# Part 1, second half, of layer 2's output product: from direct matmuls to seven products of half size, mixed step by step with part 2's

## The chip, the cores and the metric

The kernel runs on one core of one Trainium2 chip. The metric is the device time of one execution in microseconds (us): the median of three runs is 2115.03 us (2114.95 to 2115.57). A profile was taken of one more execution, of 2114.73 us. Its traced span is 2113.0 us; 1.73 us lie outside the span.

## The reference, cut to what matters

Two decoder layers run over 512 tokens with 2048 features. Layer 1 mixes tokens by retention, layer 2 by latent attention. What the change touches is the last product of layer 2 and what follows it:

```python
y = (jax.nn.silu(g) * o) @ w_out        # layer 2: (512 x 2048) @ (2048 x 2048)
x = x + gate * y                        # residual, after the last layer
return rmsnorm(x, final_norm_g)
```

All of it is in float32.

## The kernel before

**Numbers.** TensorE is fed float32 values as two rounded parts, a high and a low one: ScalarE (ACT) casts the high part, VectorE (DVE) subtracts it from the value to get the low part. This pair of operations is `split`, L134 to L136. One product of a weight block with an activation block is three matmuls: high by high, high by low, low by high. In the ordinary form these three stand on L158, L159 and L160; in the form with seven products they stand on one line, L984.

**Tiling.** In `w_mla_out` the 2048 output columns are cut into four parts of T = 512; H = 256 is half of that and P = 128. The output is held transposed: a block of 128 output columns by 512 tokens fills one PSUM bank and has a number kt from 0 to 15; part r holds kt 4r to 4r+3. The inputs of the product are 16 k-tiles of 128 rows by 512 tokens, in eight units of two.

- Parts 0 and 1 (`for r in range(2)`, L2540) are computed directly. A unit u loads a weight block `o2_w{r}_{u}` of 2 k-tiles by 512 columns (512 KB) into one of three buffers with the tag "raw", splits it, and takes 2 k-tiles x 4 blocks x 3 = 24 matmuls of 512 columns of tokens.
- Part 2 (`o2_2`, made by `seven_rows_steps`, L966) uses the seven products of Strassen and Winograd in place of eight: the weights of a step are a 2 x 2 pattern (even and odd k-tiles, left and right 256 columns), the tokens are in two halves. Eight steps `00` to `03` and `10` to `13` follow one another. A step of the first four loads two tiles of 512 KB, `e` and `o`, forms differences on DVE (L1016, L1018, L1019), splits both tiles (L1017/L1020 and L1022/L1023) and takes four products of 12 matmuls of 256 columns (x, s, z, y). A step of the second four loads 768 KB, prepares them at L1028 to L1034, and takes three such products (x, y, s). Sums of the inputs, `o2_s` and `o2_t` of each of the eight input units, are formed earlier by `o2_sums` (L2408); four of the t sums are split later (`o2_late_sums`).
- Part 3 (`o2_3`, L2607) is direct again, with weight tiles `o2_w3_0` to `o2_w3_7`.

**Closing a block.** `o2_put` (L2471) adds the gated product to the residual on DVE (L2477), squares it and scales it on ACT, and adds the squares to a running sum `x2_ss` on DVE (L2489). The residual rows are loaded by `o2_residual` (L2431) into tiles `o2_xr{kt}`, five buffers with the tag "pp" for kt below 13. Finished blocks of part 1 stand in the list `waiting` and are put one by one (`put_one`).

**Order.** It is written by hand. Each engine has its queue of instructions and runs it in order. `chunk` and `run` issue load, preparation and matmuls of a unit; `o2_hooks(i)` adds other work at unit i, counted over parts 0 and 1 (16 units): sums of unit u at hook u+6, the loads of the first three steps of part 2 at hooks 13, 14 and 15. The loop at L2579 goes through the eight steps: the load of the step after the next two, some loads for part 3 (`loads3`) and one residual, all on SyncE's queue (SP), then the matmuls, then the preparation of the step after the next and the work in `work3`. Loads take their buffer by turns from the pool "bw" (two) and the pool "raw" (three), in `turns3`; a load into a buffer waits on SP until the last reader of the buffer has finished, and all that stands behind it on SP waits with it.

Of the kernel before, what the change touches and what calls it, by code (L numbers as in the profile page):

```python
# [49 lines left out]
def hybrid_trunk_kernel(  # L50
# [2402 lines left out]

# [332 lines left out]
```

## Time and profile before

| | |
|---|---|
| median of three runs | 2115.03 us (2114.95 to 2115.57) |
| profiled execution | 2114.73 us, span 2113.0 us |
| PE (matmuls) | 2098.4 us busy, 99% |
| PEld (weight loads) | 1814.2 us, 86% |
| DVE | 1680.8 us, 80% |
| ACT | 1054.1 us, 50% |
| POOL | 103.8 us, 5% |
| DMA | 465.08 MB, mean 220 GB/s |
| chain that ended last | PE 95%, DMA 3%, DVE 1% |
| part 1 direct (192 matmuls) | 1973.41 to 2016.93 |
| part 2, seven products (336 matmuls) | 2016.93 to 2055.32 |
| part 3 and the end | from 2055.32; span ends at 2113.0 |

Busy shares are means over the whole span. For one stage one reads the stretch of that stage: which engine has no gap in it, and what its rare gaps waited for. A matmul's row shows its own duration, but matmuls are pipelined, so a stream's pace is read from the distance of starts. DVE's rows overlap by some 0.08 us in the same way. SPq rows are issues of DMAs on SyncE's queue; the time from issue to landing stands in the DMA view.

### The profile page before, as it was taken

How to read it: one execution, taken by the hardware profiler on the slowest of the kernel's cores; microseconds unless marked ns; L12 is line 12 of the kernel's file. 1: busy time of each engine (PE TensorE's matmuls, PEld its weight loads, DVE VectorE, ACT ScalarE, POOL GpSimd, SP SyncE). 2: the span in 40 equal slices, each digit the busy share in tenths (PEclk: the TensorE clock that was granted, in tenths of full speed). 3: DMA queues.
4: the chain of work that ended last, by engine and by line, in shares of the span. 5: the costliest groups of instructions: out<-in, count | busy, mean ns of one | idle time of the engine just before them, and what ended most of it. 6: DMA issues, size and time to landing. Idle time of an engine off the chain costs nothing.

```text
span 2113.0 us, 30423 instructions
## 1 busy us (share of the span) xinstructions
PE 2098.4 (99%) x11268; PEld 1814.2 (86%) x11268; DVE 1680.8 (80%) x2562; ACT 1054.1 (50%) x1626; POOL 103.8 (5%) x177
## 2 busy tenths in 40 slices
PE   8999999999999999999999999999999999999998
PEld 6888898989889888888888888898889999888898
DVE  7999888888888789666777877767978788887675
ACT  6765444444444444434344445345446565665343
POOL 1001010000000000000000000010000000000000
PEclk9999999999999999999999999999999999999999
DMA  9975786868777778755656656753556655455453
GB/s 382 407 281 195 250 276 222 278 216 268 245 259 250 237 237 278 260 188 183 234 170 227 220 184 235 265 178 111 167 186 207 199 166 187 153 188 176 148 166 126
DMA packets 237303, 465.08 MB, mean 220 GB/s; under 512 B 21169, under 2 KB 91857, under 8 KB 233569
## 3 DMA queue, kind: packets, MB, share of 16 engines
q1 hardware_dynamic: 224512, 423.17, 60.5%
q0 software_dynamic: 11920, 38.91, 4.8%
q8 instruction: 88, 1.44, 0.3%
q10 hardware_dynamic: 722, 1.06, 0.2%
q14 instruction: 61, 0.50, 0.1%
HBM read 420.06 MB, written 43.00 MB: 219 GB/s over the span
## 4 chain that ended last, share of the span: by engine, by line
PE 95%; DMA 3%; DVE 1%; ACT 0%; SPq 0%; issue 0%; POOLq 0%; DVEq 0%
PE o L1486 16%; PE x L884 2%; PE x L883 2%; PE y L884 2%; PE y L883 2%; PE s L884 2%; PE s L883 2%; PE x L885 2%; PE s L885 2%; PE y L885 2%; PE o L2607 2%; PE qk L158 2%; PE s_qk L984 2%; PE x_qk L984 2%; PE qk L160 2%; PE qk L159 2%
## 5 line engine op out<-in xcount | busy, mean ns | idle before, releaser
L1486 PE MATMUL o<-o_h,o_p 128*128 128x512 f32 (+1 forms) x1088 | 322.9, 377 | 0.0
L1486 PEld LDWEIGHTS o<-o_h,o_p 128*128 128x128 f32 x1088 | 200.2, 188 | 37.1
L1486 PE MATMUL o<-o_l,o_p 128*128 128x512 f32 (+1 forms) x544 | 204.8, 377 | 0.0
L136 DVE TENSOR_TENSOR o_p<-o_r,o_p 128x1024 fp32r<-128x1024 f32 x64 | 78.1, 1221 | 52.5 <-ACT o_p L135 52.2
L1486 PEld LDWEIGHTS o<-o_l,o_p 128*128 128x128 f32 x544 | 102.3, 188 | 18.2
L1170 DVE SCALAR_TENSOR_TENSOR mod<-mod,c_odd 128x1024 f32<-128x1024 f32 x56 | 67.2, 1219 | 14.9 <-DMA mod<-in_ada_t_dram 14.9
L135 ACT CAST o_p<-o_r 128x1024 fp32r<-128x1024 f32 x64 | 66.7, 1053 | 21.3 <-PE o L1486 7.7
L158 PE MATMUL qk<-hT,qk_p 128*128 128x512 f32 x192 | 75.0, 391 | 0.0
L160 PE MATMUL qk<-hT,qk_p 128*128 128x512 f32 x192 | 74.8, 390 | 0.0
L159 PE MATMUL qk<-hT,qk_p 128*128 128x512 f32 x192 | 74.7, 389 | 0.0
L389 DVE SCALAR_TENSOR_TENSOR aw<-aw,c_all 128x2048 f32<-128x2048 f32 (+1 forms) x37 | 73.2, 1997 | 1.6 <-DMA aw<-in_ada_t_dram 1.4
L1332 ACT ACTIVATE yn<-y,nmr,gn_r 128x512 f32<-128x512 f32 x32 | 22.3, 777 | 67.7 <-DVE nmr L1326 67.7
L159 PE MATMUL o<-o_l,o_w 128*128 128x512 f32 x128 | 49.9, 390 | 0.3 <-DVE o_l L136 0.3
L158 PE MATMUL o<-o_h,o_w 128*128 128x512 f32 x128 | 50.1, 391 | 0.0
L160 PE MATMUL o<-o_h,o_w 128*128 128x512 f32 x128 | 49.9, 390 | 0.0
L1170 DVE SCALAR_TENSOR_TENSOR mod<-mod,c_bm 128x1024 f32<-128x1024 f32 x40 | 48.7, 1218 | 0.0
L448 PE MATMUL g<-hT,g_p 128*128 128x512 f32 x192 | 46.1, 389 | 0.0
L2046 PE MATMUL uv<-ukv_p,kvT 128*128 128x256 f32 x384 | 46.1, 279 | 0.0
L136 DVE TENSOR_TENSOR qk_p<-qk_r,qk_p 128x1024 fp32r<-128x1024 f32 x23 | 27.9, 1222 | 22.1 <-ACT qk_p L135 21.8
L2046 PEld LDWEIGHTS uv<-ukv_p,kvT 128*128 128x128 f32 x384 | 44.9, 189 | 0.1
L2607 PE MATMUL o<-o_h,o_w 128*128 128x256 f32 (+1 forms) x208 | 43.6, 306 | 0.0
L160 PEld LDWEIGHTS qk<-hT,qk_p 128*128 128x128 f32 x192 | 36.0, 188 | 7.8 <-DVE qk_p L136 0.3
(1735 smaller groups left out, 6308.0 us busy)
## 6 DMA issues: line engine op xcount, KB each, us to landing
mod<-in_ada_t_dram SPq DMA_DIRECT2D x96, 512.0 KB, 5.7
o_r<-in_ret_w_out_dram SPq DMA_DIRECT2D x64, 512.0 KB, 5.4
aw<-in_ada_t_dram SPq DMA_DIRECT2D x28, 1024.0 KB, 9.5
mod_gate<-in_ada_t_dram SPq DMA_DIRECT2D x32, 512.0 KB, 5.1
qk_r<-in_ret_w_in_dram SPq DMA_DIRECT2D x48, 256.0 KB, 3.2
qk_r<-qk_d SPq DMA_DIRECT2D x32, 256.0 KB, 5.9
v_r<-v_d SPq DMA_DIRECT2D x32, 256.0 KB, 5.8
sg<-g_d SPq DMA_DIRECT2D x32, 256.0 KB, 6.2
```

What stands on the lines that cost most here:

```text
L136: DVE.tensor_sub(lo, src, hi.bitcast(F32))
L158: PE.matmul(o, lhs[0], rhs[0], start=first and not seeded, stop=False, skip_group_check=seeded)
L159: PE.matmul(o, lhs[0], rhs[1], start=False, stop=False, skip_group_check=seeded)
L160: return PE.matmul(o, lhs[1], rhs[0], start=False, stop=last, skip_group_check=seeded)
L883: PE.matmul(banks[b], a[0], w[0], start=first, stop=False, skip_group_check=True)
L884: PE.matmul(banks[b], a[0], w[1], start=False, stop=False, skip_group_check=True)
L885: PE.matmul(banks[b], a[1], w[0], start=False, stop=True, skip_group_check=True)
L984: PE.matmul(o, w[wp][:, i, b * P : (b + 1) * P], a[ap], start=first and i + b + k == 0, stop=k == 2, skip_group_check=True,)
L1170: DVE.scalar_tensor_tensor(out=aw, in0=aw, scalar=1.0, in1=silu_c[j], op0=ALU.mult, op1=ALU.mult, accum_out=row_sums[piece][:, j, b : b + 1],)
L1486: PE.matmul(o, w[i][:, ki, c0 + b * P : c0 + (b + 1) * P], a[j], start=first and i + j == 0, stop=last and i == 1, skip_group_check=True,)
L2046: PE.matmul(ps[:, (t % 2) * 256 : (t % 2 + 1) * 256], a[i], w[k], start=t % 2 + i + k == 0 and kt == 1, stop=kt == 3 and i == 1, skip_grou ...
L2607: PE.matmul(banks3[b][:, cols], last_w[u][i][:, ki, b * P : (b + 1) * P], o2_moving(2 * u + ki, cols)[j], start=u + ki + i + j == 0, stop= ...
```

## The change

Only the second half of part 1 (columns T+H to 2T, kt 6 and 7) is computed otherwise. It becomes seven products of half size by a new function, `seven_half_steps`, named `o2_1h`: eight steps as in part 2, but with 128 instead of 256 columns on each side of the weights' pattern, so 24 matmuls of 256 columns of tokens in each of the first four steps and 18 in each of the second four. A first step loads 512 KB, a second step 384 KB (its last quarter in rows of 512 bytes), into one tile of the same buffers. Two banks hold its four sums, x with s and z with y.

The first half of part 1 (kt 4 and 5) stays direct, but in four weight blocks of 4 k-tiles by 256 columns instead of eight of 2 by 512; a block still has 24 matmuls.

The steps of part 2 and the new half steps (h in what follows) take turns in `turns7`: 00, h00, 01, h01, and so on to 12, h12, h13, 13. The sums of the inputs move from hooks 6 to 13 to hooks 5 to 11, the first loads of the steps to hooks 9, 10 and 11 (there are twelve units now), the residual loads to other steps, and the work in `work3` behind the half steps.

```diff
     def o2_residual(kt):
-        tag, bufs = ("sg", 3) if kt >= 13 else ("pp", 5)
+        tag, bufs = ("sg", 3) if kt >= 13 else ("rot", 2) if kt == 11 else ("pp", 5)
...
-        if 5 < i < 14 and sums3[2 * (i - 6)] is None:
-            with behind(V_, A_):
-                o2_sums(i - 6)
-        if i in (13, 14, 15):
+        for u in {5: (0,), 6: (1, 2), 7: (3,), 8: (4,), 9: (5,), 10: (6,), 11: (7,)}.get(i, ()):
+            if sums3[2 * u] is None:
+                with behind(V_, A_):
+                    o2_sums(u)
+        if i in (9, 10, 11):
             with behind(S_):
-                seven[i - 13].units[0][0]()
-                if i == 14:
-                    for kt in range(4, 8):
+                turns7[i - 9][0].units[0][0]()
+                if i == 10:
+                    for kt in (4, 5):
                         o2_residual(kt)
-        if i == 15:
+        if i == 11:
...
-            wt = load_w([(whole, rows(w_mla_out, u, 2, r * T, T))], 2, T, f"o2_w{r}_{u}")
+            kn = 2 * r + 2
+            wt = load_w([(whole, rows(w_mla_out, u, kn, r * T, T // (r + 1)))], kn, T // (r + 1), f"o2_w{r}_{u}")
...
+    def seven_half_steps(name, c0, finish):
...
+            def load():
+                src = w_mla_out[:, c0 : c0 + H].rearrange("(u i e p) n -> u e p i n", i=2, e=2, p=P)[u]
+                w["raw"] = turns3[0]([P, 2, T], n).rearrange("p e (i n) -> p e i n", i=2)
+                if not second:
+                    for e in range(2):
+                        nc.sync.dma_start(w["raw"][:, e], src[e])
+                else:
+                    nc.sync.dma_start(w["raw"][:, 0], src[1])
+                    nc.sync.dma_start(w["raw"][:, 1, 0].rearrange("p (i n) -> p i n", i=2), src[0, :, :, P:])
...
+                    DVE.tensor_sub(t3, r[:, 0, :, P:], t3)
+                    hl = seven_parts([P, 3 * H], n, ASIDE)
+                    split(r.rearrange("p e i n -> p (e i n)")[:, : 3 * H], *hl)
...
+            def follow():
+                if not second and u == 3:
+                    m1, held["m"] = tmp(f"m1_{name}"), tmp(f"m_{name}")
+                    ACT.copy(m1[:, :H], held["x"])
+                    DVE.tensor_add(held["y"], held["y"], m1[:, :H])
+                    ACT.copy(held["m"][:, H:], held["s"])
+                    DVE.tensor_add(held["s"], held["y"], held["m"][:, H:])
...
+    halves7 = seven_half_steps("o2_1h", T + H, half_finish)
+    turns7 = [(steps7[j], j, end) for j in range(8) for end, steps7 in enumerate((seven, halves7))]
+    turns7[14:] = [(halves7[7], 7, 0), (seven[7], 7, 1)]
...
-    for j, step in enumerate(seven):
+    for m, (step, j, end) in enumerate(turns7):
         with behind(S_):
-            if j + 3 < 8:
-                seven[j + 3].units[0][0]()
-            for u in loads3.get(j, ()):
-                last_load(u)
-            if j > 3:
-                o2_residual(4 + j)
+            if m + 3 < len(turns7):
+                turns7[m + 3][0].units[0][0]()
+            if not end:
+                for u in loads3.get(j, ()):
+                    last_load(u)
+                for kt in {3: (6, 7), 4: (8,), 5: (9,), 6: (10,), 7: (11,)}.get(j, ()):
+                    o2_residual(kt)
         with behind(T_):
             step.multiply()
...
-            if j + 2 < 8:
-                seven[j + 2].units[0][1]()
-            work3.get(j, lambda: None)()
+            if m + 2 < len(turns7):
+                turns7[m + 2][0].units[0][1]()
+            if end:
+                work3.get(j, lambda: None)()
```

Three places in the order. The first is SP's queue in part 1, where `o2_w1_` is a direct weight block of part 1, `o2_2_00e` and `o2_2_00o` are the two tiles of part 2's first step, and `o2_1h_00` is the tile of the first half step. Before:

```order
L142 DMA o2_w1_4_raw_18442<-in_mla_w_out_dram 128x2x512
L1009 DMA o2_2_00o_r_18483<-in_mla_w_out_dram 128x2x256 x2
L1009 DMA o2_2_00e_r_18480<-in_mla_w_out_dram 128x2x256 x2
L142 DMA o2_w1_5_raw_18486<-in_mla_w_out_dram 128x2x512
L1009 DMA o2_2_01o_r_18518<-in_mla_w_out_dram 128x2x256
L1009 DMA o2_2_01e_r_18515<-in_mla_w_out_dram 128x2x256 x2
```

Now, on the same queue:

```order
L142 DMA o2_w1_0_raw_18306<-in_mla_w_out_dram 128x4x256
L1009 DMA o2_2_00o_r_18347<-in_mla_w_out_dram 128x2x256 x2
L1009 DMA o2_2_00e_r_18344<-in_mla_w_out_dram 128x2x256 x2
L2403 DMA o2_in7_18237<-o2_d_68 128x2x512
L142 DMA o2_w1_1_raw_18350<-in_mla_w_out_dram 128x4x256
L2434 DMA o2_xr4_18391<-x1_d_66 128x512
L2565 DMA o2_1h_00_r_18388<-in_mla_w_out_dram 128x2x256 x2
L142 DMA o2_w1_2_raw_18395<-in_mla_w_out_dram 128x4x256
L2434 DMA o2_xr5_18393<-x1_d_66 128x512
L1009 DMA o2_2_01e_r_18433<-in_mla_w_out_dram 128x2x256 x2
L1009 DMA o2_2_01o_r_18436<-in_mla_w_out_dram 128x2x256 x2
L142 DMA o2_w1_3_raw_18448<-in_mla_w_out_dram 128x4x256
```

The loads of the first steps now stand among the first of four direct blocks, no longer among the last of eight; the last direct block, `o2_w1_3`, is loaded into the buffer that `o2_2_00e` held.

The second place is DVE's queue at the end of the direct matmuls of part 1 (L136 is the split's subtraction). Before:

```order
L136 TENSOR_TENSOR o2_w1_5_18488<-o2_w1_5_raw_18486,o2_w1_5_18488 128x1024
L136 TENSOR_TENSOR o2_s7_18477<-o2_s7f_18471,o2_s7_18477 128x2x256
L136 TENSOR_TENSOR o2_w1_6_18531<-o2_w1_6_raw_18529,o2_w1_6_18531 128x1024
L1016 TENSOR_TENSOR o2_2_00e_r_18480<-o2_2_00e_r_18480 128x2x256
L1018 TENSOR_TENSOR o2_2_00o_r_18483<-o2_2_00o_r_18483,o2_2_00e_r_18480 128x2x256
L1019 TENSOR_TENSOR o2_2_00o_r_18483<-o2_2_00o_r_18483 128x2x256
L1020 TENSOR_TENSOR o2_2_00e_18564<-o2_2_00e_r_18480,o2_2_00e_18564 128x1024
L1023 TENSOR_TENSOR o2_2_00o_18570<-o2_2_00o_r_18483,o2_2_00o_18570 128x1024
L136 TENSOR_TENSOR o2_w1_7_18575<-o2_w1_7_raw_18573,o2_w1_7_18575 128x1024
```

Now (of the sums, the last rows only; the sums of units 4 to 7 stand between `o2_w1_2` and `o2_2_00e`, 16 additions or subtractions of 256 columns and 4 splits of 512, with one `x2_ss`):

```order
L2419 TENSOR_TENSOR o2_t7f_18425<-o2_in7_18237,o2_s7f_18424 128x256
L136 TENSOR_TENSOR o2_s7_18430<-o2_s7f_18424,o2_s7_18430 128x2x256
L1016 TENSOR_TENSOR o2_2_00e_r_18344<-o2_2_00e_r_18344 128x2x256
L1018 TENSOR_TENSOR o2_2_00o_r_18347<-o2_2_00o_r_18347,o2_2_00e_r_18344 128x2x256
L1019 TENSOR_TENSOR o2_2_00o_r_18347<-o2_2_00o_r_18347 128x2x256
L1020 TENSOR_TENSOR o2_2_00e_18439<-o2_2_00e_r_18344,o2_2_00e_18439 128x1024
L1023 TENSOR_TENSOR o2_2_00o_18445<-o2_2_00o_r_18347,o2_2_00o_18445 128x1024
L136 TENSOR_TENSOR o2_w1_3_18450<-o2_w1_3_raw_18448,o2_w1_3_18450 128x1024
L2574 TENSOR_TENSOR o2_1h_00_r_18388<-o2_1h_00_r_18388 128x2x128
```

The last direct block's split stands behind part 2's first step in both, but it is now the fourth block and not the eighth, and there is no direct block between the sums and that step.

The third place is SP's queue and DVE's at the last half step, `o2_1h_13` (`o2_xr9` is the residual of kt 9, `o2_w3_` a tile of part 3). SP now:

```order
L2567 DMA o2_1h_12_r_18975<-in_mla_w_out_dram 128x2x256
L2568 DMA o2_1h_12_r_18975<-in_mla_w_out_dram 128x2x128
L2658 DMA o2_w3_2_r_18980<-in_mla_w_out_dram 128x2x512
L2434 DMA o2_xr9_18982<-x1_d_66 128x512
L2567 DMA o2_1h_13_r_19027<-in_mla_w_out_dram 128x2x256
L2568 DMA o2_1h_13_r_19027<-in_mla_w_out_dram 128x2x128
L1009 DMA o2_2_13o_r_19058<-in_mla_w_out_dram 128x2x256 x2
```

DVE now, around the split of half step 12 and the put of kt 4 (`x2_2`, which reads `o2_xr4`):

```order
L136 TENSOR_TENSOR o2_t6_18932<-o2_t6f_18380,o2_t6_18932 128x2x256
L136 TENSOR_TENSOR o2_t7_18935<-o2_t7f_18425,o2_t7_18935 128x2x256
L1030 TENSOR_TENSOR o2_2_11e_r_18853<-o2_2_11o_r_18850,o2_2_11e_r_18853 128x512
L1031 TENSOR_TENSOR o2_2_11o_18938<-o2_2_11o_r_18850,o2_2_11o_18938 128x1024
L1034 TENSOR_TENSOR o2_2_11e_18942<-o2_2_11e_r_18853,o2_2_11e_18942 128x512
...
L1031 TENSOR_TENSOR o2_2_12o_19020<-o2_2_12o_r_18947,o2_2_12o_19020 128x1024
L1034 TENSOR_TENSOR o2_2_12e_19024<-o2_2_12e_r_18950,o2_2_12e_19024 128x512
L2584 TENSOR_TENSOR o2_1h_12_r_18975<-o2_1h_12_r_18975 128x256
L136 TENSOR_TENSOR o2_1h_12_19049<-o2_1h_12_r_18975,o2_1h_12_19049 128x768
L2479 SCALAR_TENSOR_TENSOR x2_2_19052<-o2_1_0_18304,gate_c1_93,o2_xr4_18391 128x512
```

The residual of kt 9 takes the buffer of `o2_xr4`, so on SP it waits for that put; the last half step's load and part 2's last loads stand behind it. Before, SP's queue had `o2_xr9` behind all loads of part 2:

```order
L2434 DMA o2_xr8_18879<-x1_d_66 128x512
L2558 DMA o2_w3_0_r_18877<-in_mla_w_out_dram 128x2x512
L1009 DMA o2_2_13e_r_18875<-in_mla_w_out_dram 128x2x256
L2558 DMA o2_w3_1_r_18932<-in_mla_w_out_dram 128x2x512
L2558 DMA o2_w3_2_r_18934<-in_mla_w_out_dram 128x2x512
L2434 DMA o2_xr9_18936<-x1_d_66 128x512
```

There nothing of part 2 stands behind `o2_xr9`.

## Rows read from the trace of the kernel before

**Rows 1.** Page, part 1: busy time, share of the span, instructions

```profile
PE 2098.4 (99%) x11268; PEld 1814.2 (86%) x11268; DVE 1680.8 (80%) x2562; ACT 1054.1 (50%) x1626; POOL 103.8 (5%) x177
```

**Rows 2.** Longest wait of PE from 1900 to 2113: total, times, longest (us)

```profile
PE o L159 <- DVE o_l L136: 0.3, 1, 0.3
```

**Rows 3.** Timeline of PE at 1973, 1783 and 2017: start, us, what

```profile
1973.41 0.39 PE L158 MATMUL o<-o_h,o_w 128*128 128x512 f32 x1
...
1782.95 5.77 PE L2046 MATMUL uv<-ukv_p,kvT 128*128 128x256 f32 x48
1788.56 0.39 PE L158 MATMUL o<-pt,v 128*128 128x512 f32 x1
...
2016.93 0.28 PE L984 MATMUL x_o<-o_h,o_00e 128*128 128x256 f32 x1
```

**Rows 4.** Chain that ended last, 2010 to 2060: start, us, what

```profile
2053.96 1.36 PE y_o L984 x12
2055.32 4.81 PE o L2607 x21
```

**Rows 5.** Timeline of DVE from 1975 to 1981

```profile
1975.34 1.22 DVE L136 TENSOR_TENSOR o_w<-o_w_raw,o_w 128x1024 fp32r<-128x1024 f32 x1 [0.26 <-ACT o_w L135]
1976.48 0.42 DVE L2418 TENSOR_TENSOR o_t5f<-o_in 128x256 f32<-128x256 f32 x1
1976.82 0.68 DVE L2489 TENSOR_TENSOR x_ss<-x_ss,x_sq 128x512 f32<-128x512 f32 x1
1977.42 0.41 DVE L2416 TENSOR_TENSOR o_s2f<-o_in 128x256 f32<-128x256 f32 x1
```

**Rows 6.** Timeline of DVE, ACT and SP's queue from 2000 to 2011

```profile
2001.41 0.68 DVE L1016 TENSOR_TENSOR o_00e_r<-o_00e_r 128x512 f32<-128x512 f32 x1
...
2003.46 1.22 DVE L1020 TENSOR_TENSOR o_00e<-o_00e_r,o_00e 128x1024 fp32r<-128x1024 f32 x1
...
2004.71 0.37 SPq L142 DMA_DIRECT2D o_w_raw<-in_mla_w_out_dram  x1
...
2008.44 1.05 ACT L135 CAST o_w<-o_w_raw 128x1024 fp32r<-128x1024 f32 x1 [3.74 <-DMA o_w_raw<-in_mla_w_out_dram]
...
2009.53 1.23 DVE L136 TENSOR_TENSOR o_w<-o_w_raw,o_w 128x1024 fp32r<-128x1024 f32 x1 [3.57 <-ACT o_w L135]
```

**Rows 7.** DMA view, 1965 to 2060: issues, KB each, median us to landing

```profile
o_w_raw<-in_mla_w_out_dram SPq DMA_DIRECT2D x5, 512.0 KB, 3.9
...
o_01o_r<-in_mla_w_out_dram SPq DMA_DIRECT2D x2, 256.0 KB, 4.8
...
o_12o_r<-in_mla_w_out_dram SPq DMA_DIRECT2D x2, 256.0 KB, 4.2
...
o_12e_r<-in_mla_w_out_dram SPq DMA_DIRECT2D x1, 256.0 KB, 2.7
```

**Rows 8.** Timeline of DVE, ACT and SP's queue from 2037 to 2050

```profile
2037.68 0.59 ACT L991 COPY m_o<-s_o 128x512 f32<-128x512 f32 x1 [2.13 <-PE s_o L984]
...
2038.91 0.68 DVE L1030 TENSOR_TENSOR o_11e_r<-o_11o_r,o_11e_r 128x512 f32<-128x512 f32 x1
2039.51 1.22 DVE L1031 TENSOR_TENSOR o_11o<-o_11o_r,o_11o 128x1024 fp32r<-128x1024 f32 x1
...
2048.04 0.75 DVE L2477 SCALAR_TENSOR_TENSOR x<-o,gate_c,o_xr 128x512 f32<-128x512 f32 x1
...
2048.82 0.34 SPq L2434 DMA_DIRECT2D o_xr<-x_d  x1
```

**Rows 9.** Windows: PE, PEld, DVE, ACT, POOL busy, PE clock, DMA share, GB/s

```profile
1990.00:2000.00 10.00, 10.00 (x46) 8.29 (x45) 3.28 (x7) 2.39 (x3) 0.00 (x0) 1.00 0.79 267
...
2109.00:2110.00 1.00, 0.00 (x0) 0.00 (x0) 0.00 (x0) 0.00 (x0) 0.00 (x0) 1.00 1.10 338
2110.00:2111.00 1.00, 0.00 (x0) 0.00 (x0) 0.00 (x0) 0.00 (x0) 0.00 (x0) 0.51 0.91 219
```

**Rows 10.** Timeline of PE from 2105 on: its last matmuls

```profile
2104.74 1.15 PE L2715 MATMUL y_ps<-ident,x 128*128 128x128 f32 x9
```

More of the change, by code (lines that the diff above doesn't have):

```diff
@@ L2538, in hybrid_trunk_kernel, with product, step, prepare @@
     )
+    def seven_half_steps(name, c0, finish):
+        held = {}
+        def product(bank, n, u, w, first):
+            for i in range(2):
+                p = 2 * u + i
+                if isinstance(n, tuple):
+                    a = tuple(o2_hl[(2 * p + n[0]) // 2][h][:, n[0], n[1] * H : (n[1] + 1) * H] for h in range(2))
+                else:
+                    a = tuple(sums3[2 * p + (n - 1) // 2][:, (n - 1) % 2, h, :] for h in range(2))
+                for k, (wp, ap) in enumerate(((0, 0), (0, 1), (1, 0))):
+                    PE.matmul(bank, w[wp][:, i], a[ap], start=first and i + k == 0, stop=k == 2, skip_group_check=True)
+        def step(second, u):
+            n = f"{name}_{int(second)}{u}"
+            w = {}
+            def load():
[4 more added lines that the diff above has]
+                        nc.sync.dma_start(w["raw"][:, e], src[e])
+                else:
+                    nc.sync.dma_start(w["raw"][:, 0], src[1])
+                    nc.sync.dma_start(w["raw"][:, 1, 0].rearrange("p (i n) -> p i n", i=2), src[0, :, :, P:])
+            def prepare():
+                r = w["raw"]
+                if not second:
+                    e0, e1, o0, o1 = (r[:, e, :, j * P : (j + 1) * P] for e in range(2) for j in range(2))
+                    DVE.tensor_sub(e1, e1, e0)
+                    DVE.tensor_sub(o1, o1, e1)
+                    DVE.tensor_sub(o0, o0, o1)
+                    hl = seven_parts([P, 2, T], n, ASIDE)
+                    split(r.rearrange("p e i n -> p e (i n)"), *hl)
+                    hl = [t.rearrange("p e (i n) -> p e i n", i=2) for t in hl]
+                    for k, (e, j) in {"b11": (0, 0), "t1": (0, 1), "t4": (1, 0), "t2": (1, 1)}.items():
+                        w[k] = tuple(t[:, e, :, j * P : (j + 1) * P] for t in hl)
+                else:
+                    t3 = r[:, 1, 0].rearrange("p (i n) -> p i n", i=2)
+                    DVE.tensor_sub(t3, r[:, 0, :, P:], t3)
+                    hl = seven_parts([P, 3 * H], n, ASIDE)
+                    split(r.rearrange("p e i n -> p (e i n)")[:, : 3 * H], *hl)
+                    for k, j in (("b21", 0), ("b22", 1)):
+                        w[k] = tuple(
+                            t[:, : 2 * H].rearrange("p (i n) -> p i n", i=2)[:, :, j * P : (j + 1) * P] for t in hl
+                        )
+                    w["t3"] = tuple(t[:, 2 * H :].rearrange("p (i n) -> p i n", i=2) for t in hl)
+            def multiply():
+                if not second and u == 0:
+                    for j, keys in enumerate(("xs", "zy")):
+                        held[j] = aux(f"{name}_{keys}")
+                        for h, k in enumerate(keys):
+                            held[k] = held[j][:, h * H : (h + 1) * H]
+                if not second:
+                    forms = [("x", (0, 0), "b11"), ("s", 1, "t1"), ("z", (1, 1), "t4"), ("y", 2, "t2")]
+                    if u == 3:
+                        forms = [forms[i] for i in (0, 3, 1, 2)]
+                else:
+                    forms = [("x", (1, 0), "b21"), ("y", 3, "t3"), ("s", 4, "b22")]
+                    if u == 3:
+                        forms = [forms[i] for i in (0, 2, 1)]
+                for k, f, key in forms:
+                    product(held[k], f, u, w[key], not second and u == 0 and k in "xz")
+            def follow():
[5 more added lines that the diff above has]
+                    DVE.tensor_add(held["s"], held["y"], held["m"][:, H:])
+                if second and u == 0:
+                    ACT.copy(held["m"][:, :H], held["z"])
+                if second and u == 3:
+                    finish(held["x"], held["s"], held["y"], held["m"])
+            return Step(load, prepare, multiply, follow)
+        return [step(second, u) for second in (False, True) for u in range(4)]
@@ new lines, in half_finish @@
+    def half_finish(x, s, y, m):
+        m2 = m.rearrange("p (a n) -> p a n", a=2)
+        DVE.tensor_add(m2, m2, y.unsqueeze(1).to_broadcast([P, 2, H]))
+        for j, ps in enumerate((x, s)):
+            parts = list(zip((ps, m2[:, j]), both_halves))
+            waiting.append(lambda kt=6 + j, parts=parts: o2_put(kt, parts)())
+    halves7 = seven_half_steps("o2_1h", T + H, half_finish)
+    turns7 = [(steps7[j], j, end) for j in range(8) for end, steps7 in enumerate((seven, halves7))]
+    turns7[14:] = [(halves7[7], 7, 0), (seven[7], 7, 1)]
@@ L2542, in hybrid_trunk_kernel @@
             chunk(
-                [(lambda u=u: o2_unit(r, u), [2 * u, 2 * u + 1]) for u in range(KD // 2)],
-                [(acc, aux)[r](f"o2_{r}_{b}") for b in range(4)],
+                [
+                    (lambda u=u: o2_unit(r, u), list(range((2 * r + 2) * u, (2 * r + 2) * (u + 1))))
+                    for u in range(KD // (2 * r + 2))
+                ],
+                [(acc, aux)[r](f"o2_{r}_{b}") for b in range(4 - 2 * r)],
                 lambda w, ki, kt, b: w_block(w, ki, b), lambda w, ki, kt, b: o2_moving(kt),
```

7 lines of the change are left out of this document (4 added, 3 removed).

## The prediction

> **What bounds the kernel now.** The page's first part says PE is busy 99% of the span [rows 1]; that is a mean, so I went on to the view of PE's waits for the last 213 us: nothing longer than 0.3 us [rows 2]. From there the chain of waits is PE alone, one stream after another, until the last rows are written [rows 4]. So in the stretch that the change touches time is the number of matmuls times their pace, plus any wait that the change brings in. The page's busy shares of DVE, ACT and SP say nothing on that; it needs the timelines of DVE and SP's queue around the moved work [rows 5, 6 and 8], the DMA view [rows 7] and the windows [rows 9].
>
> **PE's own work.** Part 1's direct stream starts at 1973.41 and part 2 at 2016.93 [rows 3]: 43.52 us for 192 matmuls of 512 columns, 0.2267 each. A form of part 2 takes 1.36 for 12 of 256 columns [rows 4], 0.1133 each. The direct form loses half of its matmuls, 96 x 0.2267 = 21.76. The eight half steps add 4 x 24 + 4 x 18 = 168 of 256 columns, 168 x 0.1133 = 19.04. Gain: **2.72 us**. The bound on the other side is the one place where 48 matmuls of 256 columns ran slower: 1782.95 to 1788.56, 0.1169 each [rows 3]; with it the gain is 2.1. I take 2.72, since the half steps have the form of part 2's.
>
> One rule speaks against trading one long matmul for two short ones. The Trainium skill, "TensorE: Matmul & The Clock Gate", section "Back-to-back issue gap", holds that in a stream of weight load and matmul the spacing is set by both, and gives about 81 ns for 128 columns and 131 ns for 512: a shorter matmul then saves less than its share of columns. An estimate halfway between its two figures in columns, 98 ns for 256, would turn the change into 168 x 0.098 - 96 x 0.131, a loss of 3.9. The trace doesn't agree: 256 columns cost exactly half of 512 here, 0.1133 to 0.2267, with a weight load for each matmul in both.
>
> **Direct block 4 (`o2_w1_3`).** PE needs it after three blocks of 24 matmuls: 1973.41 + 3 x 5.44 = 1989.73. Its load goes into the buffer of `00e`, so SP can issue it only after DVE's L1020 of `00e`. DVE's queue up to there: the split of `o2_w1_2` stands behind the last put of part 0 in both orders, 1975.34, and the next operation starts at 1976.48 [rows 5]. Now come one x_ss of 0.60, 16 half-width operations of 0.34 and four splits of 0.60 (distances of starts in [rows 5]): 8.44, to 1984.92. L1016 to L1020 take 2.05 and SP's issue follows L1020's start by 1.25 [rows 6]: issued at 1988.22. From issue to cast 3.73, cast 1.05, from the cast's start to the split 1.09 and the split 1.23 [rows 6]: high part ready at 1993.00, low part at 1994.27. PE waits 1993.00 - 1989.73 = 3.3; the third matmul of the block needs the low part and would come at 1993.45, so 0.8 more: **+4.1 us**. In the kernel before the same wait exists, but the block behind it is the eighth, due at 1973.41 + 7 x 5.44 = 2011.5 with its split starting at 2009.53. The cover was two direct blocks longer. Bounds: a load in rows of 1 KB took 4.8 in place of 3.9 [rows 7], 0.9 more; a load as fast as 2.7 gives 1.2 less. So 2.9 to 5.0. Behind the wait `h00`'s preparation is late by as much as PE; I count nothing twice.
>
> **Half step h13.** Its load stands on SP behind `o2_xr9`, which takes the buffer of `o2_xr4`, and so waits for the put of kt 4 on DVE, which stands behind `h12`'s split. Count from the moment t0 at which PE starts half step h03. Its s form ends after 18 matmuls, 2.04. The copy of 256 columns, about 0.4 (512 take 0.59 [rows 8]), then L2616 of half width: DVE is free at 3.0. `h10`: subtraction 0.42, cast of 768 columns 0.82 (between 0.59 and 1.05 [rows 6, 8]), split 0.95 (between 0.68 and 1.23): 5.25. Two late sums' splits and L1030 at 0.60 each, L1031 of `11o` 1.22 [rows 8]: 8.27. The load of `12o` takes the buffer of `11o` and lands 4.2 later [rows 7]: 12.5. Cast 1.05, L1031 1.2, L1034 0.60, `h12`'s subtraction, cast and split 2.2: 17.55. Put 0.75, `o2_xr9`'s issue 0.34 [rows 8]: h13's load issues at 18.65. Its second piece follows 0.4 later, and I give it 3.3, between the 2.7 and the 4.2 of the DMA view [rows 7]: landed 22.4. Subtraction, cast and split: high part at 23.7, low part at 24.65. PE comes to h13 after the last 6 matmuls of h03 and after 10, h10, 11, h11, 12 and h12: 6 x 0.1133 + 3 x (36 + 18) x 0.1133 = 19.04, so at t0 + 2.04 + 19.04 = 21.08. It waits 2.6 for the high part, 0.7 for the low one, and some 0.6 in step 13, whose tiles are loaded and prepared behind h13's: **+4.0 us**. With 2.7 for both loads in this chain it is 1.9, with 4.8 for both 5.4.
>
> **What costs nothing.** Counting the order, DVE gains 25 instructions and SP 7. Between 1990 and 2000 DVE is busy 3.28 of 10 us [rows 9], and PE has a block's preparation two steps ahead. The sums' earlier hooks fall beside part 0's and part 1's matmuls, the loads of 00, h00 and 01 find their buffers free. Half steps h00 to h03 and h10 to h12 come out at least 1.5 us early by the same count (h12's split at 17.55 against 19.0). If that cover fails, it costs as much as it falls short; I have put it in the range. The banks of the half form are freed by the copies at L2614 to L2616 and by the puts of kt 6 and 7, which come in time for part 3. From part 3 on the work is the old one.
>
> **Sum.** -2.72 + 4.1 + 4.0 = +5.4. On the profiled execution's 2114.73 (its span and 1.73 outside) that is 2120.1; its time is 0.30 below the median shown, so the forecast is **2120.4 us**. Own range of this case: -2.72 (or -2.1) with 2.9 to 5.0 and 1.9 to 5.4, not all ends together: 2117.8 to 2123.0.
>
> **Rivals.**
> A, the cover holds in both places, and PE runs through: 2115.03 - 2.72 = 2112.3, faster than before by 0.13%. It speaks for it that DVE idles two thirds of 1990 to 2000 [rows 9], that is, the old order had slack. Against it: the stretch ahead is the one that counts, and there DVE's queue is a chain of rows without gaps. The mechanism decides at 3.3 us: if DVE reached L1020 of `00e` that much earlier, block 4 would be in time.
>
> B, only one of the two waits comes, the other is covered by something that the count has too long (the load of h13, or DVE's row of sums): 2115.03 - 2.72 + 4.0 = 2116.3. For it: both margins are made of loads of 2.7 to 4.8 us, and each is 3 us on a chain of 20.
>
> C, both waits come and TensorE's clock falls to its lower level in them. The granted clock before is 1.00 up to the window from 2109 to 2110 and 0.51 after it [rows 9], while the last matmul ends at 2105.89 [rows 10], so some 4 us without a matmul pass before it falls. My waits are of 3.3 and 0.8, 2.6 and 0.7 us with matmuls between, shorter than that. If it fell, matmuls would run at 1.2 in place of 2.4 GHz; 4 us of work at half pace, as long as PE stood, would add some 4: 2124.4. The Trainium skill, same page, section "Part 1: The HAM clock gate", says that the throttled state is the default and that activity releases it; no run here shows a wait as short as these lowering the clock.
>
> D, no wait comes, but the weight loads set the pace of the short matmuls. At the slowest row for this size, 0.1169 [rows 3], all 504 of the mixed stretch take 504 x 0.0036 = 1.8 more, and the time is 2115.03 - 2.72 + 1.8 = 2114.1. Part 2's own rows [rows 4], in the same form, speak against it. By the figures of the rule on the gap (the Trainium skill, same page as above) it would be 2115.03 + 3.9 = 2118.9.
>
> **How the numbers follow.** The forecast 0.60, A 0.12, B 0.20, C 0.07, D 0.01. What a measurement of this kernel tells from no change is 0.2%, 4.2 us: faster below 2110.8, slower above 2119.3. A and B lie within; A reaches faster only if a gain appears that no row shows, 0.02 in all. Of the forecast's 0.60, ends of 2117.8 and 2123.0, about three quarters lie above 2119.3, 0.46, with C 0.07 and a little of B with a longer wait, 0.02: slower 0.55, same 0.43. The range: 2114.0 leaves out A, and 2123.5 leaves out C's upper half and the last of the forecast: about 0.2.
>
> **What would show it.** In the new profile's waits of PE: a wait at L158 for the cast of `o2_w1_3` of about 3.3 us and one at L160 of about 0.8; SP's issue of that load just behind DVE's L1020; part 1's direct stream ending some 4 us later than 1973.41 + 21.76 = 1995.17. Then a wait at the half steps' matmul line for h13 of 2.6 and of 0.7, `o2_xr9`'s issue just behind the put of kt 4, and part 3 starting near 2055.32 + 5.4 = 2060.7. The half steps' pace of 0.1133 shows the first term. The forecast is wrong if block 4's load is issued before DVE reaches L1020 of `00e`, if 12o's load does not wait for `11o`, or if a wait shows at a step where I count none.

## The result, and the profile after

The changed kernel takes 2125.47 us (median of four runs, 2123.13 to 2126.08), the one before 2114.99: 1.0047 times as long, with an interval of 1.003 to 1.0064. It is slower by 10.5 us; the forecast was 2120.4 with a range to 2123.5. The profile is of the fastest of the four, 2123.13 us with a span of 2121.4, 8.4 more than before; that one execution lies inside the range, the median 2.0 above its end.

PE's busy time has hardly moved (page, part 1):

```profile
PE 2100.0 (99%) x11340; PEld 1818.6 (86%) x11340; DVE 1693.8 (80%) x2587; ACT 1060.4 (50%) x1633; POOL 104.0 (5%) x177
```

72 matmuls more, as counted, and still 99%: again a mean that hides what happened. PE's waits from 1900 on, which were nothing over 0.3 before [rows 2], show it:

```profile
PE o_1h_xs L2554 <- ACT o_1h L135: 3.2, 1, 3.2
PE o L158 <- ACT o_w L135: 2.8, 1, 2.8
PE x_sums L2751 <- ACT x_sq L2486: 0.2, 1, 0.2
```

Both forecast waits are there. The timeline of all engines around the first, with the same operations as [rows 6]:

```profile
1986.69 1.22 DVE L1020 TENSOR_TENSOR o_00e<-o_00e_r,o_00e 128x1024 fp32r<-128x1024 f32 x1
...
1987.94 0.37 SPq L142 DMA_DIRECT2D o_w_raw<-in_mla_w_out_dram  x1
...
1991.36 1.04 ACT L135 CAST o_w<-o_w_raw 128x1024 fp32r<-128x1024 f32 x1 [3.44 <-DMA o_w_raw<-in_mla_w_out_dram]
...
1992.44 1.23 DVE L136 TENSOR_TENSOR o_w<-o_w_raw,o_w 128x1024 fp32r<-128x1024 f32 x1 [3.26 <-ACT o_w L135]
1992.46 0.50 PE L158 MATMUL o<-o_h,o_w 128*128 128x512 f32 x1 [2.84 <-ACT o_w L135]
```

SP issues block 4's load just as `00e` is released, 1987.94 (1988.22 was forecast), and everything else follows from that. The timeline around the second:

```profile
2046.17 0.96 DVE L136 TENSOR_TENSOR o_1h<-o_1h_r,o_1h 128x768 fp32r<-128x768 f32 x1 [0.94 <-ACT o_1h L135]
2047.04 0.75 DVE L2479 SCALAR_TENSOR_TENSOR x<-o,gate_c,o_xr 128x512 f32<-128x512 f32 x1
...
2047.82 0.34 SPq L2434 DMA_DIRECT2D o_xr<-x_d  x1
2048.25 0.39 SPq L2567 DMA_DIRECT2D o_1h_r<-in_mla_w_out_dram  x1
...
2053.66 0.58 PE L2554 MATMUL o_1h_xs<-o_h,o_1h 128*128 128x256 f32 x1 [3.25 <-ACT o_1h L135]
...
2054.62 0.37 SPq L1009 DMA_DIRECT2D o_13e_r<-in_mla_w_out_dram  x1
...
2059.95 0.69 DVE L1034 TENSOR_TENSOR o_13e<-o_13e_r,o_13e 128x512 fp32r<-128x512 f32 x1
...
2061.39 1.58 PE L984 MATMUL y_o<-o_t,o_13e 128*128 128x256 f32 x12
...
2062.80 0.40 PE L2710 MATMUL o<-o_h,o_w 128*128 128x512 f32 x1
```

h12's split, the put of kt 4, the residual, h13's load: the forecast chain, link by link. But part 3 starts at 2062.80 where 2060.7 was forecast. One part of the picture is in the windows behind that wait (columns as in [rows 9]):

```profile
2051.00:2052.00 1.00, 0.00 (x0) 0.00 (x0) 0.00 (x0) 0.00 (x0) 0.00 (x0) 1.00 0.74 236
...
2053.00:2054.00 1.00, 0.34 (x1) 0.35 (x2) 0.36 (x1) 1.00 (x2) 0.00 (x0) 0.50 0.26 91
...
2058.00:2059.00 1.00, 1.00 (x7) 1.00 (x6) 0.56 (x2) 0.00 (x0) 0.00 (x0) 0.50 0.00 0
...
2060.00:2061.00 1.00, 1.00 (x11) 1.00 (x10) 1.00 (x2) 0.97 (x2) 0.00 (x0) 1.00 0.43 90
```

TensorE ran nothing for 3.2 us, and the granted clock fell to its lower level of 1.2 GHz for some 7 us (the windows 2052 to 2053 and 2059 to 2060 have means of 0.83 and 0.76, those between 0.50): rival C. The Trainium skill, "TensorE: Matmul & The Clock Gate", section "Part 1: The HAM clock gate", calls the throttled state the default that activity lifts; the trace agrees: the clock fell with nothing running and rose after matmuls. The 4 us read from [rows 9 and 10] were no safe bound.

All kernels are compared below by three distances of PE's and DVE's timelines: when part 2's first matmul starts (no wait in block 4: 1995.4 to 1995.8), how long the mixed stretch from there to part 3 takes (504 matmuls, 57.12 at 0.1133), and how long from part 3's start to the first row of the last output rows (48.24 before). Distances are of one trace each; the ratio is to the kernel before as measured beside each run (medians of 2114.86 to 2115.19).

| kernel | median, us | ratio to before | part 2 starts | mixed stretch | part 3 |
|---|---|---|---|---|---|
| before | 2114.99 | | 2016.93 | | 48.24 |
| changed | 2125.47 | 1.0047 (1.0030 to 1.0064) | 1998.39 | 64.41 | 48.23 |
| e0, changed again | 2125.83 | 1.0051 (1.0036 to 1.0066) | 2000.68 | 65.10 | 49.18 |
| e1, block 4 mended | 2120.59 | 1.0027 (1.0016 to 1.0038) | 1995.82 | 63.61 | 48.54 |
| e2, h13 mended | 2121.77 | 1.0031 (1.0018 to 1.0043) | 2000.17 | 60.55 | 48.97 |
| e3, both | 2117.67 | 1.0010 (1.0001 to 1.0019) | 1995.61 | 61.20 | 48.80 |
| e4, and part 3's loads later | 2117.18 | 1.0009 (1.0000 to 1.0018) | 1995.55 | 58.21 | 51.30 |
| e5, matmuls in the wait (28 more in the stretch) | 2125.29 | 1.0049 (1.0035 to 1.0063) | 2001.02 | 64.23 | 48.99 |
| e6, e4 and sums later | 2116.90 | 1.0008 (1.0000 to 1.0017) | 1995.63 | 57.69 | 51.48 |
| e7, e6 and puts first | 2114.05 | 0.9996 (0.9987 to 1.0005) | 1995.37 | 57.70 | 48.20 |
| e8, e7 but the put of kt 4 | 2113.89 | 0.9994 (0.9986 to 1.0003) | 1995.81 | 57.68 | 48.17 |
| e9, e8 and a tile's place | 2114.94 | 1.0001 (0.9991 to 1.0010) | 1995.80 | 59.36 | 48.18 |

### The profile page after: what moved, and what is told of

The parts are those of the page before. It is cut to its first block, busy times and chain, and to the rows that moved or that the text cites. A ratio compares the mean times of both kernels' runs of the same rounds, so it can differ in the third digit from the quotient of the medians.

```text
span 2121.4 us, 30626 instructions
## 1 busy us (share of the span) xinstructions
PE 2100.0 (99%) x11340; PEld 1818.6 (86%) x11340; DVE 1693.8 (80%) x2587; ACT 1060.4 (50%) x1633; POOL 104.0 (5%) x177
## 4 chain that ended last, share of the span: by engine, by line
PE 93%; DMA 3%; DVE 2%; ACT 1%; issue 1%; SPq 0%; DVEq 0%; POOLq 0%; ACTq 0%
PE o L1486 16%; PE x L884 2%; PE x L883 2%; PE y L884 2%; PE y L883 2%; PE s L884 2%; PE s L883 2%; PE x L885 2%; PE y L885 2%; PE s L885 2%; PE o L2710 2%; PE qk L158 2%; PE s_qk L984 2%; PE x_qk L984 2%; PE qk L160 2%; PE qk L159 2%
## 5 line engine op out<-in xcount | busy, mean ns | idle before, releaser
L136 DVE TENSOR_TENSOR o_p<-o_r,o_p 128x1024 fp32r<-128x1024 f32 x64 | 78.2, 1223 | 52.8 <-ACT o_p L135 52.8
L136 DVE TENSOR_TENSOR qk_p<-qk_r,qk_p 128x1024 fp32r<-128x1024 f32 x23 | 27.9, 1223 | 22.1 <-ACT qk_p L135 21.9
L160 PEld LDWEIGHTS qk<-hT,qk_p 128*128 128x128 f32 x192 | 36.0, 188 | 7.8 <-DVE qk_p L136 0.3
L158 PEld LDWEIGHTS qk<-hT,qk_p 128*128 128x128 f32 x192 | 36.0, 188 | 7.8 <-ACT g_st L474 0.5
L448 PEld LDWEIGHTS g<-hT,g_p 128*128 128x128 f32 x192 | 36.0, 188 | 7.5
L159 PEld LDWEIGHTS qk<-hT,qk_p 128*128 128x128 f32 x192 | 36.1, 188 | 7.3
```

The source lines that it names most:

```text
L158: PE.matmul(o, lhs[0], rhs[0], start=first and not seeded, stop=False, skip_group_check=seeded)
L159: PE.matmul(o, lhs[0], rhs[1], start=False, stop=False, skip_group_check=seeded)
L160: return PE.matmul(o, lhs[1], rhs[0], start=False, stop=last, skip_group_check=seeded)
```

## The experiments

**e0, the changed kernel again.** No edit.

> The changed kernel once more, for a second trace: the executions so far gave 2123.1, 2125.2, 2125.8 and 2126.1 us, and the profile is of the fastest. Theory (two late loads, and the clock at half after the second): the same two waits of about 2.8 and 3.2 us, the granted clock 0.5 for some 6 us after the second, span about 2121 to 2124. What the slower executions lose beyond that is open: either the clock falls after the first wait too (then 0.5 stands behind 1992), or the two loads land later (then a wait is 2 us longer at a clock of 1.00 after the first).

The trace, of a run of 2127.09 us, has both waits (2.9 and 4.0), and the clock falls after the first too. Windows inside and behind that wait:

```profile
1991.00:1992.00 1.00, 0.00 (x0) 0.00 (x0) 0.00 (x0) 0.00 (x0) 0.00 (x0) 1.00 0.90 311
1994.00:1995.00 1.00, 1.00 (x4) 0.72 (x4) 1.00 (x2) 0.00 (x0) 0.00 (x0) 0.50 0.01 2
1997.00:1998.00 1.00, 1.00 (x6) 0.80 (x5) 0.87 (x1) 0.10 (x1) 0.00 (x0) 1.00 0.49 172
```

A wait of 2.84 left the clock at 1.00, one of 2.9 did not. Against the first trace part 2 starts 2.3 later: 1.0 of that is there before the change begins (the put of kt 2 starts at 1973.01, not 1971.98), 1.3 is the clock. So these two executions differ in whether the first wait, too, is followed by the low clock, and in how long the loads take.

**e1, block 4's load mended.** Step 01's load moves behind it, and block 4 gets the buffer of `o2_w1_2`.

```diff
-        if i in (9, 10, 11):
+        if i in (9, 10):
...
+        if (r, u) == (1, 3):
+            with behind(S_):
+                turns7[2][0].units[0][0]()
```

> Only the first load is mended: the loads of step 01 are issued behind the load of direct block 4 (o2_w1_3), so that this block takes the buffer of o2_w1_2 and no longer waits for VectorE's work on step 00. Theory: the first wait (2.8 us and 0.5 of the low part) goes, all else stays: 3.3 us less than the changed kernel, near 2119.8 for an execution like the profiled one, and the second wait with its half clock stays. Rival (the loads share one limit, and what is gained is waited for at the next late load): the second wait grows by 3 us and the time stays at 2123 to 2126.

Part 2 starts at 1995.82 with no wait, and the median is 5.2 us below that of e0, more than the 3.3 of a wait without the low clock; the second wait stays 3.2, with the low clock behind it. The rival falls: the two waits are separate. Not all else stayed, though: behind the second wait the clock is low for some 3.4 us in place of 7, and the mixed stretch is 0.8 shorter than in the first trace.

**e2, h13's load mended.** The residual of kt 9 is issued one step later.

```diff
-                for kt in {3: (6, 7), 4: (8,), 5: (9,), 6: (10,), 7: (11,)}.get(j, ()):
+                for kt in {3: (6, 7), 4: (8,), 6: (9, 10), 7: (11,)}.get(j, ()):
```

> Only the second load is mended: the residual of kt 9 is issued one step later, so that half step 13's load no longer stands behind a wait for the put of kt 4. Theory: that load issues at about 2044.6 instead of 2048.3, the wait at h13 falls from 3.2 to under 0.8 us, the clock stays at 1.00, so 2.5 to 3.2 of the wait and 2.9 of the clock go, with 0.6 at step 13: about 2116.5 to 2117.5. Rival (the half clock isn't due to this wait): only the wait goes and the time is near 2119.8.

The wait falls from 3.2 to 0.5 and the clock stays at 1.00 there, but the median is 2121.77, 4.1 below e0 where 6 were expected (the first wait is as it was, with the low clock behind it: part 2 starts at 2000.17). The mixed stretch is 3.9 shorter than in the first trace, and not 6, so neither theory has the number. New waits stand in step 13 (PE's waits):

```profile
PE o_1h_xs L2554 <- DVE o_1h L136: 0.5, 1, 0.5
PE y_o L984 <- ACT o_13e L1033: 0.4, 1, 0.4
...
PE y_o L984 <- DVE o_13e L1034: 0.2, 1, 0.2
```

**e3, both edits.**

> Both loads are mended (the two edits together). Theory: PE runs through but for some tenths; the time is the one before less the 2.72 us of matmuls: 2112.3 to 2113.2, faster than before by 0.1%. Rival (the mixed order has a cost of its own, in late steps or at the end): 2115 or more.

2117.67: the rival. With both forecast waits mended the change still loses 2.5 us (2115.19 beside it), at a clock of 1.00 to the end of part 3. The timeline at step 13:

```profile
2047.77 0.96 DVE L136 TENSOR_TENSOR o_1h<-o_1h_r,o_1h 128x768 fp32r<-128x768 f32 x1 [0.94 <-ACT o_1h L135]
...
2048.76 0.37 SPq L1009 DMA_DIRECT2D o_13e_r<-in_mla_w_out_dram  x1
...
2053.41 0.69 DVE L1030 TENSOR_TENSOR o_13e_r<-o_13o_r,o_13e_r 128x512 f32<-128x512 f32 x1 [1.19 <-DMA o_13e_r<-in_mla_w_out_dram]
...
2054.80 0.51 PE L984 MATMUL y_o<-o_t,o_13e 128*128 128x256 f32 x2 [0.81 <-ACT o_13e L1033]
```

`13e` takes h13's raw buffer, so its load cannot be issued before h13's split, and arrives 4.6 us later. A third late load, by the same rule as the first two. From h13's first matmul to part 3 the 54 matmuls take 9.02 (2047.79 to 2056.81), where 54 at 0.1178 are 6.4.

**e4, part 3's loads later**, on top of e3, so that the last steps find free buffers:

```diff
-    loads3 = {4: (0,), 5: (1, 2), 6: (3,), 7: (4, 5)}
+    loads3 = {5: (0,), 6: (1, 2), 7: (3, 4, 5)}
```

> Both loads mended, and part 3's loads put off by a step (part 3's tiles 0, then 1 and 2, then 3 to 5 at steps 11, 12 and 13), so that the last steps of part 2 and of the half find a free buffer. With both loads mended PE still lost 4.1 us between step 00 and part 3 (61.20 us for 504 matmuls, 57.12 at 0.1133): 1.2 at h13 and 1.8 in step 13, whose tile 13e was issued only behind h13's split, the rest in a slower pace of 0.118 from step 11 on. Theory: the buffers are what the last steps wait for; with them free the waits at h13 and 13e go, 2.5 to 3 us: 2114.5 to 2115.3. Rival (VectorE's own queue is what is late there): the waits stay within 0.5 us of what they were, 2117 to 2118.

The mixed stretch falls by 3.0 as the theory has it, yet the time only to 2117.18: part 3 takes 2.5 longer. In the trace of e6, which has the same, the timeline shows why:

```profile
2048.80 0.37 SPq L2661 DMA_DIRECT2D o_w_r<-in_mla_w_out_dram  x1
...
2053.71 1.22 DVE L136 TENSOR_TENSOR o_w<-o_w_r,o_w 128x1024 fp32r<-128x1024 f32 x1 [3.20 <-ACT o_w L135]
...
2060.56 0.50 PE L2713 MATMUL o<-o_h,o_w 128*128 128x512 f32 x1 [1.27 <-DVE x L2482]
```

DVE stands 3.2 us for part 3's tile 1, and the puts that free part 3's banks stand behind it. The wait had moved.

**e5, matmuls in the wait.** The changed kernel with 28 matmuls that the result doesn't use ahead of h13's.

```diff
+            if m == 14:
+                for _ in range(28):
+                    PE.matmul(
+                        seven_z["o2_2"][0][:, :H], o2_hl[0][0][:, 0, :P], o2_hl[0][0][:, 0, :H], start=True, stop=True,
+                        skip_group_check=True,
+                    )
             step.multiply()
```

> The changed kernel with 28 matmuls of 256 columns more, just ahead of half step 13's on TensorE's queue, into a bank that is no longer read; they do no work for the result and take 3.2 to 3.3 us, as long as the wait at h13. Nothing of the loads is changed. Theory (the clock falls because TensorE stands): the granted clock stays at 1.00 from 2050 to 2063, and half step 13 and step 13 run at 0.118 a matmul and not at 0.21, 2.5 to 3.5 us less: 2122 to 2123.5. Rival (the low clock comes from something else, or the late loads alone cost the time): the clock still falls and the time is at or above that of the changed kernel, 2125 to 2127.

Half of each. The clock stays at 1.00 through that place, as the theory has it, and falls as before after the first wait, which has no filling (windows):

```profile
1995.00:1996.00 1.00, 1.00 (x3) 0.81 (x4) 0.93 (x3) 0.00 (x0) 0.00 (x0) 0.50 0.04 11
2051.00:2057.00 6.00, 5.99 (x51) 5.79 (x49) 2.42 (x4) 2.34 (x3) 0.00 (x0) 1.00 0.64 198
2057.00:2063.00 6.00, 4.29 (x35) 3.88 (x34) 4.14 (x5) 2.43 (x3) 0.00 (x0) 1.00 0.16 47
```

But the time is that of the changed kernel. The 54 matmuls of h13 and 13 take 9.10 us at full clock (2056.15 to 2065.25) and took 9.14 in the first trace, mostly at half (2053.66 to 2062.80): now PE waits for `13o` (1.0 and 0.8) and `13e` instead.

```profile
2058.49 1.04 ACT L1031 CAST o_13o<-o_13o_r 128x1024 fp32r<-128x1024 f32 x1 [2.04 <-DMA o_13o_r<-in_mla_w_out_dram]
```

This alone doesn't show that the low clock is free, since the second half of `13o` landed 6.3 us after its issue here, and no half of it took more than 4.9 in the first trace (the tile's view). The rows of `13e` tell more. In e0 its low part is ready at 2064.44 and PE, with the low clock behind it, is at the form that reads it before that:

```profile
2063.75 0.69 DVE L1034 TENSOR_TENSOR o_13e<-o_13e_r,o_13e 128x512 fp32r<-128x512 f32 x1
...
2064.09 1.85 PE L984 MATMUL y_o<-o_t,o_13e 128*128 128x256 f32 x12
```

There the low clock cost nothing; part 3 starts 1.34 behind the low part, as it does in e5. In the first trace the low part is ready at 2060.64 and PE comes to that form only at 2061.39, late by its slow matmuls; 1.34 behind 2060.64 would have been 2061.98, so an estimate of the clock's cost there is 0.8. The low clock ran beside loads that were late anyway, and cost what they didn't hide.

**e6, the last two sums' splits later**, on top of e4:

```diff
-    early3 = {2: lambda: (o2_late_sums(4), o2_late_sums(5)), 4: lambda: (o2_late_sums(6), o2_late_sums(7))}
+    early3 = {2: lambda: (o2_late_sums(4), o2_late_sums(5)), 5: lambda: (o2_late_sums(6), o2_late_sums(7))}
```

> As the one with part 3's loads put off, and the splits of the last two sums (t6 and t7) moved behind step 11's preparation on VectorE, so that the low part of 11o comes 1.2 us earlier. In all four traces so far TensorE waits some 0.2 us for it in the first form of step 11, and from there on every matmul of 256 columns takes 0.1178 in place of 0.1133, to the end of step 13. Theory A (the short wait takes TensorE's lead in weight loads, and the stream never gets it back): step 11 and what follows run at 1.36 for 12, and 0.3 + 162 x 0.0045 = 1.0 us goes. Theory B (the slower pace belongs to the place, by what the matmuls read or write there): 1.41 stays, and only the 0.3 goes.

The chain of waits of e4 at step 11:

```profile
2034.62 1.63 PE x_o L984 x12
2036.26 1.41 PE y_o L984 x12
2037.67 1.41 PE s_o L984 x12
```

and of e6:

```profile
2034.70 1.36 PE x_o L984 x12
2036.06 1.36 PE y_o L984 x12
2037.42 1.37 PE s_o L984 x12
```

Theory A in its main point: without the wait of 0.3 the pace stays, up to h13, where some 0.2 is waited and 0.1178 follows again. So the mixed stretch is 0.5 shorter, not 1.0, and the medians (2116.90 and 2117.18) don't tell the two apart. That a stream "never gets it back" is wrong: in e5 the same wait is followed by 1.36, and only the next by 1.41.

**e7 and e8, the order on DVE**, on top of e6; e8 is e7 with the put of kt 4 where it was.

```diff
-        5: put_one, 6: lambda: (last_prepare(0), last_prepare(1), put_one()),
-        7: lambda: (put_one(), put_one(), last_prepare(2)),
+        6: lambda: (put_one(), last_prepare(0), put_one()),
+        7: lambda: (put_one(), put_one(), last_prepare(1), last_prepare(2)),
```

> As the one with the last sums later, and two places moved on VectorE's queue: the put of kt 4 behind half step 13's preparation, and the split of part 3's tile 1 behind the puts of kt 6 and 7. In the trace of the one before it TensorE ran from step 00 to part 3 in 57.69 us (57.12 at 0.1133), but part 3 up to the last rows took 51.48 us where the kernel before takes 48.24: VectorE stood 3.2 us for part 3's tile 1, whose load came late, and the puts of kt 6 and 7, which free the banks of part 3, stood behind it. Theory (a late tile holds up whatever stands behind it on VectorE; matmuls saved come out once none is late): part 3 takes 48.3 again and h13's wait of 0.9 goes: 2111.8 to 2113, faster than before by 2 to 3 us. Rival (the saved matmuls don't shorten the time; some other tile is late next): 2114.5 or more.

> As the last one, but the put of kt 4 stays where it was, ahead of half step 13's preparation. Theory: part 3 takes 48.3 us, h13 still waits 0.6 to 0.9 us and the stream behind it keeps the pace of 0.1178 for its 54 matmuls (0.2 us): 0.8 to 1.1 us more than with the put moved too. Rival (the put's place is nothing, the wait at h13 comes from its load): the same time as the other within 0.4 us.

Part 3 is back at 48.2 in both, and PE's waits are gone but for this in e7:

```profile
PE x_sums L2754 <- ACT x_sq L2489: 0.2, 1, 0.2
PE x_o L984 <- DVE o_13o L1031: 0.2, 1, 0.2
```

They beat the changed kernel by 11.4 and 11.6 us in the medians. Against the one before (2115.18 beside them) they are 1.1 and 1.3 ahead, inside the interval: not told from no change, and e7 doesn't meet the 2 to 3 us expected. The put's place is worth nothing: what e7 gains at h13 it waits for `13o`, which its own put holds up on DVE. In e7's trace the last output rows start at 2101.27, 2.1 before those of the kernel before (2103.40), and the span ends only 0.7 earlier: from these rows to the end it takes 11.0 us, not 9.6.

**e9, a tile's place.** The parts of `00e` at offset 0.

```diff
-        lambda second, u: 0, ((False, 0),),
+        lambda second, u: 0, (),
```

> As the one before (part 3's tile 1 behind the puts), and the parts of tile 00e are placed at offset 0 of their buffer, as those of all later steps are, where so far this one tile lay 64 bytes further. Its 24 matmuls have taken 1.43 and 1.44 for 12 in every trace, the kernel's before too, those of the next forms 1.36. Theory A (the slower pace of 0.119 is the start of a stream of 256-column matmuls behind one of 512 columns, or any wait): 1.43 stays in the first two forms. Theory B (it is the place of the weights): 1.36 from the first form on, 0.15 us less, which a time can't tell.

Neither. The chain of waits from the start of part 2:

```profile
1995.96 1.41 PE x_o L984 x12
1997.38 1.41 PE s_o L984 x12
1998.79 1.41 PE z_o L984 x12
```

and so to the end of step 13, with no wait in it: the mixed stretch takes 59.36 and not 57.68. The median is 1.05 above e8's, so the runs without a trace point the same way.

## Why the prediction was wrong

**The gain was right on PE.** The half steps ran at 0.1133 up to the first wait, and e7 and e8, in which nothing of note is late, need 57.7 for the mixed stretch against 57.12 counted; part 3 starts 2.1 and 1.7 earlier there than before. In the whole time a gain isn't shown. (The prediction's 98 ns is a third of the way between its two figures, not halfway; nothing hangs on it.)

**Block 4's wait was right in its mechanism and nearly in its size.** 2.84 for the high part and some 0.4 for the low: against [rows 3] part 2 should start at 1995.17 and starts at 1998.39, 3.2 late, where 4.1 was forecast; the load took 3.4 to the cast where 3.73 was put. e1 shows it is that load alone. In three of the four traces that have this wait the low clock follows it; in e0 it adds 1.3.

**The step that failed is h13's, at its end: "some 0.6 in step 13, whose tiles are loaded and prepared behind h13's".** The wait at h13 itself was 3.25 (2.6 and 0.7 forecast). The mixed stretch, though, lost 64.41 - 57.12 = 7.3, and not 4.0. Of the rest some 2.8 are step 13, from h13's first matmul on: 54 matmuls that take 6.4 at 0.1178 took 9.1. Its tile `13e` takes the buffer that h13's split frees, so load (4.0), subtraction, cast and split start only then, 1 us after PE starts h13, and need 6 us, 7 in all, while PE has 42 matmuls, 4.9 us, from that start to the first that reads `13e`. Both numbers stood in the rows ([rows 7 and 8]); I had followed the chain to h13 and put a guess on the next link. By the estimate under e5 the late tiles are 2.0 of the 2.8 and the low clock 0.8. e3 shows the link without the low clock: 2.7 lost there, with both forecast waits mended and a load of `13e` of 4.6.

Another 1.0 is step 11, where none was counted: a wait of 0.27 for the low part of `11o`, and 162 matmuls at 0.1178. The count had that part at t0 + 8.27, 0.6 ahead of PE's first matmul of the step at t0 + 8.84. PE came as counted, but the part was ready at t0 + 9.14:

```profile
2028.46 0.28 PE L2554 MATMUL o_1h_xs<-o_h,o_1h 128*128 128x256 f32 x1
...
2031.45 0.43 DVE L2614 TENSOR_TENSOR o_1h_zy<-o_1h_zy,m_o_1h 128x256 f32<-128x256 f32 x1 [0.50 <-ACT m_o_1h L2615]
2031.99 0.43 DVE L2616 TENSOR_TENSOR o_1h_xs<-o_1h_zy,m_o_1h 128x256 f32<-128x256 f32 x1
2032.33 0.42 DVE L2584 TENSOR_TENSOR o_1h_r<-o_1h_r 128x256 f32<-128x256 f32 x1
...
2036.38 1.22 DVE L1031 TENSOR_TENSOR o_11o<-o_11o_r,o_11o 128x1024 fp32r<-128x1024 f32 x1
...
2037.31 0.28 PE L984 MATMUL x_o<-o_h,o_11o 128*128 128x256 f32 x1
```

With t0 at 2028.46, DVE is free at t0 + 3.87 and not at 3.0: the kernel closes the first four half steps with two copies and two additions (L2613 to L2616), and the count had one of each. The same 0.9 runs on down the chain to h13's load, part of why that wait was longer than forecast.

**Rival C came, but not at its price.** The clock fell, after waits shorter than the bound that I had read from [rows 9 and 10]; that "shorter than that" was the reason for 0.07. Its cost was not 4: 1.3 behind the first wait where it followed it (e0), and behind the second some 0.8 in the first trace and nothing in e0. B and A had the cover where there was none.

**Summed up for the profiled execution:** -2.72 + 3.2 + 7.1 (the 7.3 less the 0.16 that part 2 lost in the kernel before, too) = 7.6, the distance from 2055.16 to 2062.80; 0.8 more pass at the end, between the last output rows and the end of the span. That this execution lies inside the range is luck in part: block 4's wait fell 0.9 short and hid some of the rest. The median is 2.3 above it; e0's trace, 3.9 above it in the span, has 1.3 by the low clock behind the first wait, 0.7 in the mixed stretch and 0.9 in part 3, and 1.0 from ahead of the change. Where the 0.8 at the end comes from isn't settled: e6 has 0.2 of it, e7 1.4, and no run was made for it.

## What to carry to other kernels

When a load waits for a buffer, follow the ring of buffers (the few buffers that loads take by turns) to the last user and set each tile's arrival against the due time of its consumer; a chain that makes one tile late makes the next in the same ring late by its own load, and mending one wait uncovers the next (four in a row here, from 2125.8 to 2113.9). Work that is taken off a bound engine shortens the time only if every load, put and split that was timed to the old pace moves with it; here even then what is left of the gain is too small to be told. On an in-order queue put what waits longest for its input last: a residual load and one split each held up what PE needed.

## What was not expected of the hardware

**Matmuls of 256 columns have two paces at the same clock.** 0.1133 and 0.1178 each, PE and PEld both without gaps and the granted clock at 1.00 in both. Behind the first 24, which run at 0.1195 in all traces but e9's, a stream of the kernel's own matmuls kept its pace until a wait; behind a wait, one of 0.2 or 0.3 us too, either came. In e9's trace the stream took the slower one from its first matmul to its last, 504 of them, 1.7 us in the mixed stretch, and the edit had only put one tile's parts 64 bytes lower; e8, with that tile at its old place, ran at 0.1133 behind its first 24 up to h13. What sets the pace is open.

**The clock may fall to half behind a wait of 2.9 us, in some executions and not in others**, and it stayed there for some 3.4 us (e0, e1) or 7 us (first trace). It cost what the next tile's arrival didn't hide.

**A wait on SP's queue holds what stands behind it even where that has its buffer.** The Trainium skill, "DMA: Bandwidth & Descriptors", section "Anatomy of one DMA — SWDGE (gpsimd) path", says that a semaphore is waited for on the sequencer that issues, not in the DMA engine (the section describes DMAs issued by GpSimd; these are issued by SyncE). The trace agrees: h13's load takes a buffer that DVE's split of `12e` (L1034) frees. In the changed kernel that split ends at 2044.56 and the load is issued at 2048.25, 0.43 after the residual; in e3, where the residual stands behind it, the split ends at 2041.49 and the load is issued at 2041.52.
